# A gMLP and dilated-attention trunk on one core: large-tile subtractions and sums on DVE instead of GpSimd, and the last output weights gated and split ahead

## The chip, the cores and the metric

The kernel runs on one core of a Trainium2 chip. The metric is the device time of one execution, in microseconds, and the time of a kernel is the median of its runs. In the profile the engines are PE (TensorE), DVE (VectorE), ACT (ScalarE), POOL (GpSimd) and SP (SyncE); SP's queue issues all of this kernel's loads and stores.

## What is computed

A residual stream of 2048 tokens by 1024 goes through one gated MLP layer (A) and one layer of dilated attention (B). The reference, cut to the parts that the text speaks of:

```python
def gmlp_layer(x, c, ...):                       # layer A
    h = rms_norm(x, norm_g) * (1 + scale) + shift
    u, v, z = jnp.split(h @ w_in, 3, axis=-1)    # 3 x 2048 columns
    u = jax.nn.gelu(u)
    v = rms_norm(jax.nn.gelu(v), sgu_g)
    mixed = jnp.einsum('gts,bcsge->bctge', w_causal, v) + b_s   # chunks of 128
    y = u * mixed * jax.nn.silu(z)
    return x + gate * (y @ w_out)

def dilated_layer(x, c, kv_groups, ...):         # layer B
    h = rms_norm(x, norm_g) * (1 + scale) + shift
    qz = h @ w_in                                # 24 query heads of 128, and z
    for g, (window, d) in enumerate(((128, 1), (512, 4), (2048, 16))):
        o, lse = dilated_group_attn(q[g], kb[g], vb[g], slopes[g], window, d)
    alpha = jax.nn.softmax(jnp.stack(lses), axis=0)
    y = jnp.sum(alpha * o, axis=0) * jax.nn.silu(z)
    return x + gate * (y @ w_out)
```

Each band of attention sees 256 keys: the 128 of its own block up to the diagonal, and the 128 of the block before from the diagonal on.

## The kernel before

Every large product is made of two fp32r parts of each operand. A weight tile of 128x512 is loaded (256 KB), ACT copies it to the high part (`split`, L255) and DVE or POOL subtracts that from the original to get the low part (L259); high and low lie side by side in one slot of the weight pool, eight slots in all. A product is then three matmuls, high·high, high·low and low·high (`mm3`, L303 to L305; L343 to L345 for the feature-major blocks).

The 2048 tokens run in four quarters of 512, Q = 0 to 3. In each, layer A makes the blocks v (4), u (8) and z (8), the spatial mix, and the output product; then `proj_B` makes the keys and values (kv, blocks 2, 1, 0), the queries (q blocks 2, 1, 0) and z of layer B, with the parts of attention that need later tokens deferred. The q and z blocks, and the output product of Q = 1 to 3, go through `dense_s`, which makes one 2x2 block product from seven smaller ones instead of eight. For that it needs sums and differences of weights and of activations: `combine_weights` (L398) and `combine_out` (L350) make those of the weights once and keep them in DRAM (`wt`, `wq`); `make_ops` (L622) and the class `OutOperands` (L891) make those of the activations in each quarter. In the output product the order of the seven products is 11, s2, 12, s3, s1, 22, s4, and their operands are built shortly ahead of them.

Two of the four combined output weights (`wq`, i = 1 and 2) are kept split for every second row block: in Q = 0's output stage `combine_out` writes the halves into a slot of the weight pool (`wso`, L381 and L382) and stores 512 KB to `wqs`; the later output stages load these with one 512 KB transfer and no split. The other row blocks are loaded raw.

Work that belongs to no block of its own is written as generators, "fillers", which are advanced a step at a time between matmuls (`tick`, at a rate): the sums for the gates, `combine_weights`, the norm of the next quarter, and attention. During layer A of Q = 1 to 3 the filler is `attend_local(Q - 1, wrap=True)`: the 128x256 probabilities of two heads make one chunk (`pr`), with the columns of the block before and of the own block. In a wrapped unit the two halves are folded: POOL multiplies the previous half by the identity (`dg`, L1176), blanks it at and under the diagonal (L1177) and adds it to the own half (L1179); PE transposes the sum (L1196); DVE separates the two halves by a triangular mask out of PSUM (L1200, L1202), and POOL adds the diagonal back (L1203). There are 76 such chunks.

At the end `finish` runs: in the last z block (Q = 3) the fillers are `first()`, which makes the weights of the three groups and prepares the first output tile (`prepare(0)`), and `both()`, which loads layer B's output weights in 16 tiles (`rawo`) and splits them on ACT and POOL (L1293, L1294) into four large tiles `wo`. `prepare` scales and adds the three groups' outputs (DVE and ACT, L1279 to L1347) and multiplies by silu(z) (POOL, L1348). The final loop takes 16 tiles of 128 tokens: transposes (`make_yb`), two products of 24 matmuls (`pf`), then DVE multiplies the result by the gate row `gb` (L1416) and POOL adds the residual (L1417). The attention of Q = 3 is its filler.

A scheduler lists the instructions of each engine; each engine then runs its own list in order, so an instruction that waits holds up all behind it on that engine. All transfers stand on SP's queue, at most eight at a time: each issue also waits for the landing of the one eight before it.

The functions that the change touches, as they were before:

## Time and profile before

| | us |
|---|---|
| median of 3 runs | 3057.24 |
| lowest and highest run | 3051.16, 3058.77 |
| the profiled execution, its own time | 3056.17 |
| its span on the core | 3054.5 |
| PE busy in the span | 2944.3 |
| DVE busy | 2101.4 |
| ACT busy | 1668.5 |
| POOL busy | 1053.1 |

A row of the groups names the line, engine, operation, the tile written and those read, the count, then busy us and mean ns of one, then the idle time of the engine before these instructions and what ended it. In the waits, "PE pp L1196 <- POOL pr L1179: 8.0, 7, 1.5" says that PE's instruction of L1196 waited 8.0 us in all for POOL's of L1179, 7 times, 1.5 us at the longest. The granted clock is TensorE's, as a share of full speed.

### The profile page before, as it was taken

The page shows a single profiled execution, that of the slowest core. Times are in us where ns is not written, and L with a number is a line of the kernel's source. Part 1 is how long each engine was busy: PE and PEld are TensorE (multiplying, and loading weights), DVE is VectorE, ACT ScalarE, POOL GpSimd, SP SyncE. Part 2 cuts the span into 40 slices and gives each one's busy share as a digit, 9 for nine tenths or more (in the row PEclk, how much of TensorE's full clock was granted, in tenths as well). Part 3 has the DMA queues.
Part 4 walks back from the last instruction along what each step waited for, and adds up shares of the span by engine and source line. Part 5 has one row for each costly group of instructions (what it writes and reads, how often), then busy time and mean ns, then how long its engine had stood idle before and what let it go on. Part 6 is the DMA issues. An engine that isn't in the chain of part 4 may idle for free. (4 is left out here: it accounts for less than half of the span.)

```text
span 3054.5 us, 45565 instructions
## 1 busy us (share of the span) xinstructions
PE 2944.3 (96%) x14784; PEld 2465.7 (81%) x14784; DVE 2101.4 (69%) x3596; ACT 1668.5 (55%) x3398; POOL 1053.1 (34%) x1248
## 2 busy tenths in 40 slices
PE   5999989999999999999999999999999999988999
PEld 4788868788888778778888788888888788877887
DVE  6787557673468777765577776856577777767772
ACT  4323336557456555566465565566465568766540
POOL 4147354330025423433144423424145231144322
PEclk8999999999999999999999999999999999999999
DMA  7899677674433577663433676743334666778752
GB/s 235 266 310 343 236 264 258 222 246 125 139 101 116 192 251 237 219 208 104 146 94 121 195 249 206 260 155 117 120 108 135 227 218 218 224 231 290 232 166 92
DMA packets 364227, 601.33 MB, mean 197 GB/s; under 512 B 38378, under 2 KB 137932, under 8 KB 363988
## 3 DMA queue, kind: packets, MB, share of 16 engines
q1 hardware_dynamic: 363988, 598.41, 60.1%
q8 instruction: 117, 1.92, 0.3%
q14 instruction: 122, 1.00, 0.1%
HBM read 478.08 MB, written 120.20 MB: 196 GB/s over the span
## 5 line engine op out<-in xcount | busy, mean ns | idle before, releaser
L305 PE MATMUL pd_v<-w_v,hAh 128*128 128x512 f32 x1024 | 331.5, 405 | 1.2 <-ACT hAh L583 1.2
L305 PE MATMUL pd_kv<-w_kv,hkh 128*128 128x512 f32 x768 | 243.5, 397 | 5.3 <-DVE w_kv L259 4.5
L305 PEld LDWEIGHTS pd_v<-w_v,hAh 128*128 128x128 f32 x1024 | 190.3, 193 | 39.5 <-issue 1.7
L1168 ACT ACTIVATE pr<-pr,stat,rt 128x256 f32<-128x256 f32 (+1 forms) x320 | 177.4, 556 | 64.4 <-DVE stat L1162 36.2
L343 PE MATMUL pd_u<-hAh,w_u 128*128 128x512 f32 x512 | 206.1, 402 | 0.0
L343 PE MATMUL pd_z<-hAh,w_z 128*128 128x512 f32 x512 | 204.3, 399 | 0.0
L305 PE MATMUL pd_v<-w_v,hAl 128*128 128x512 f32 x512 | 203.9, 398 | 0.0
L345 PE MATMUL pd_u<-hAh,w_u 128*128 128x512 f32 x512 | 200.2, 391 | 1.6 <-DVE w_u L259 1.6
L345 PE MATMUL pd_z<-hAh,w_z 128*128 128x512 f32 x512 | 200.0, 391 | 0.0
L344 PE MATMUL pd_u<-hAl,w_u 128*128 128x512 f32 x512 | 199.6, 390 | 0.0
L344 PE MATMUL pd_z<-hAl,w_z 128*128 128x512 f32 x512 | 199.4, 390 | 0.0
L255 ACT ACTIVATE w_u<-raw_u 128x512 fp32r<-128x512 f32 x128 | 79.0, 628 | 184.7 <-PE pd_u L345 100.1
L305 PEld LDWEIGHTS pd_kv<-w_kv,hkh 128*128 128x128 f32 x768 | 145.6, 190 | 38.4 <-DVE w_kv L259 6.6
L1176 POOL TENSOR_TENSOR dg<-pr,ident 128x256 f32<-128x256 f32 x76 | 59.8, 787 | 330.0 <-ACT pr L1168 270.7
L1229 PEld LDWEIGHTS po<-kv,pT 128*128 128x128 f32 x1200 | 147.2, 191 | 8.4 <-ACT pT L1079 2.4
L305 PE MATMUL pd_kv<-w_kv,hkl 128*128 128x512 f32 x384 | 151.8, 396 | 1.0 <-DVE hkl L612 1.0
L1229 PE MATMUL po<-kv,pT 128*128 128x128 f32 x1200 | 149.7, 275 | 1.5 <-ACT pT L1079 1.5
L1014 POOL TENSOR_SCALAR s_q<-s_q 128x4 f32<-128x4 f32 x96 | 24.5, 255 | 362.0 <-DVE s_q L1013 333.4
L259 DVE TENSOR_TENSOR w_u<-raw_u,w_u 128x512 fp32r<-128x512 f32 x128 | 99.4, 787 | 72.0 <-ACT w_u L255 68.5
L1158 DVE SCALAR_TENSOR_TENSOR pr<-dist,rt,ps 128x256 f32<-128x256 f32 (+1 forms) x320 | 122.8, 430 | 34.7 <-PE ps L1155 24.6
L255 ACT ACTIVATE w_z<-raw_z 128x512 fp32r<-128x512 f32 x128 | 77.9, 625 | 123.3 <-PE pd_z L345 49.1
L259 DVE TENSOR_TENSOR w_o<-raw_o,w_o 128x512 fp32r<-128x512 f32 x104 | 92.6, 910 | 53.3 <-ACT w_o L255 53.1
(781 smaller groups left out, 8330.5 us busy)
## 6 DMA issues: line engine op xcount, KB each, us to landing
raw_q<-in_b_w_in_dram SPq DMA_DIRECT2D x144, 256.0 KB, 3.7
raw_v<-in_a_w_in_dram SPq DMA_DIRECT2D x128, 256.0 KB, 3.7
raw_u<-in_a_w_in_dram SPq DMA_DIRECT2D x128, 256.0 KB, 3.9
raw_z<-in_a_w_in_dram SPq DMA_DIRECT2D x128, 256.0 KB, 3.0
raw_o<-in_a_w_out_dram SPq DMA_DIRECT2D x104, 256.0 KB, 3.3
qt<-qd SPq DMA_DIRECT2D x96, 260.0 KB, 3.0
od<-ot SPq DMA_DIRECT2D x96, 256.0 KB, 3.9
raw_kv<-in_w_kv_dram SPq DMA_DIRECT2D x76, 256.0 KB, 3.9
```

What stands on the lines that cost most here:

```text
L255: nc.scalar.activation(hi, src, AF.Copy)
L259: e.tensor_tensor(lo, src, hi.bitcast(F32), ALU.subtract)
L305: last_mm[0] = nc.tensor.matmul(pt, a, u[:, w, :], start=f, stop=e, skip_group_check=more)
L343: nc.tensor.matmul(pts[i], wh, hh[:, k, :], start=k == 0, stop=False)
L344: nc.tensor.matmul(pts[i], wh, hl[:, k, :], start=False, stop=False)
L345: nc.tensor.matmul(pts[i], wl, hh[:, k, :], start=False, stop=k == KT - 1)
L1014: nc.gpsimd.tensor_scalar(s4[:, 4:8], s4[:, 0:4], 1.0 / P, EPS, ALU.mult, ALU.add)
L1158: nc.vector.scalar_tensor_tensor(pr[:, i, :], dist[:, 256 - w:256], u["rt"][:, h:h + 1], psc[:, i, :], ALU.mult, ALU.add)
L1168: nc.scalar.activation(pr[:, i, :], pr[:, i, :], AF.Exp, bias=mneg[:, i:i + 1], scale=u["rt"][:, h:h + 1], accum_out=lsum[:, i:i + 1])
L1176: nc.gpsimd.tensor_tensor(dg, prev, ident.unsqueeze(1).broadcast_to([P, hp, P]), ALU.mult)
L1229: nc.tensor.matmul(po[:, h * P:(h + 1) * P], u["pT"][h // hp][:, h % hp, j, :], u["kv"][:, j, kh, 1, :], start=j == 0, stop=j == nk - 1)
```

## The change

1. Large-tile subtractions, sums and products go from POOL to DVE: those of `combine_out` (32), `combine_weights` (64), `OutOperands` (30 low parts and 48 sums), `make_ops` (28 and 8), 24 of `norm_T`'s low parts, the 18 weight splits that POOL had in the output stages, the scaling of `o1` in attention (32), and the product with silu(z) in `prepare` (16). What POOL keeps are column operations of one to four elements a row, and the large ones of the opening.
2. In the wrapped attention unit the mask is gone: DVE adds the whole previous half to the own half, then makes `dg`; after the transposes DVE subtracts `dg` from the masked half before it takes the difference.
3. The combined output weights are no longer kept split: `wso` and `wqs` are gone, and the later output stages load all of `wq` raw, eight more splits in each.
4. `gate_out`, woven into the attention filler of Q = 2's layer A, loads the 16 tiles of layer B's output weights, multiplies them by the gate row on DVE, splits them (ACT, DVE) into slots of the weight pool and stores them to DRAM (`wob`, 16 transfers of 512 KB). `finish` then only loads them (`load_wo`): the first half ahead of the last q block, the second in a hook behind the fifth product of the last z block. The final loop's gate product is gone, and DVE adds the residual out of PSUM in one operation.
5. In the last z block `first()` is stretched with idle steps, and the first output tile's transposes (`opening`, `make_yb(0)`) are called inside the last product.

The diff, cut to its core:

```diff
-        split(u[:, 0, :], u[:, 1, :], raw, ordered or pool)
+        split(u[:, 0, :], u[:, 1, :], raw, ordered)
...
-        return [split_unit(rows_of(wq2[i], k // 2), f"{nm}{k}") if i in wq2 and k % 2 == 0 else
-                raw_unit(rows_of(wq[i], k), f"{nm}{k}", pool=i not in wq2 and k % 3 == 1)
-                for k in range(KT)]
+        return [raw_unit(rows_of(wq[i], k), f"{nm}{k}") for k in range(KT)]
...
             for i, t in enumerate((t1, t2, t3, t4)):
-                if k % 2 or i not in wq2:
-                    pending.append((rows_of(wq[i], k), t))
-                else:
-                    u = wp.tile([P, 2, 512], F32R, tag="w", name=f"wso{k}{i}")
-                    nc.scalar.activation(u[:, 0, :], t, AF.Copy)
-                    nc.gpsimd.tensor_tensor(u[:, 1, :], t, u[:, 0, :].bitcast(F32), ALU.subtract)
-                    pending.append((rows_of(wq2[i], k // 2), u.bitcast(F32)))
+                pending.append((rows_of(wq[i], k), t))
...
+    def gate_out():
+        items = [(n, k) for n in range(2) for k in range(KT)]
+        gb, raws, us = {}, {}, {}
+        for i in range(len(items) + 2):
...
+                raws[i] = rp.tile([P, 512], F32, tag="raw", name=f"rawo{n}{k}")
+                nc.sync.dma_start(raws[i], b_w_out[k * P:(k + 1) * P, n * 512:(n + 1) * 512])
...
+                    nc.sync.dma_start(wob[n][:, k * P:(k + 1) * P, :].rearrange("e p n -> p e n"),
+                                      us.pop(i - 2).bitcast(F32))
...
+                u = us[i - 1] = wp.tile([P, 2, 512], F32R, tag="w", name=f"w_go{n}{k}")
+                nc.vector.tensor_tensor(raw, raw, gb[n], ALU.mult)
+                nc.scalar.activation(u[:, 0, :], raw, AF.Copy)
+                nc.vector.tensor_tensor(u[:, 1, :], raw, u[:, 0, :].bitcast(F32), ALU.subtract)
...
-                nc.gpsimd.tensor_tensor(r0, r0, h0, ALU.subtract)
+                nc.vector.tensor_tensor(r0, r0, h0, ALU.subtract)
...
-                self.put("12", j, r1, nc.gpsimd if j % 4 else nc.vector)
-                nc.gpsimd.tensor_tensor(r1, r1, self.sums.pop(j), ALU.subtract)
+                self.put("12", j, r1)
+                nc.vector.tensor_tensor(r1, r1, self.sums.pop(j), ALU.subtract)
...
-                nc.gpsimd.tensor_tensor(dg, prev, ident.unsqueeze(1).broadcast_to([P, hp, P]), ALU.mult)
-                nc.gpsimd.affine_select(prev, prev, pattern=[[0, hp], [1, P]], compare_op=ALU.is_gt,
-                                        fill=0.0, base=0, channel_multiplier=-1)
-                nc.gpsimd.tensor_tensor(own, own, prev, ALU.add)
+                nc.vector.tensor_tensor(own, own, prev, ALU.add)
+                nc.vector.tensor_tensor(dg, prev, ident.unsqueeze(1).broadcast_to([P, hp, P]), ALU.mult)
...
+                nc.vector.tensor_tensor(pT[:, :, 1, :], pT[:, :, 1, :], u["dg"][:, c * hp:(c + 1) * hp, :],
+                                        ALU.subtract)
                 nc.vector.tensor_tensor(pT[:, :, 0, :], pc, pT[:, :, 1, :], ALU.subtract)
-                nc.gpsimd.tensor_tensor(pT[:, :, 0, :], pT[:, :, 0, :], u["dg"][:, c * hp:(c + 1) * hp, :], ALU.add)
...
-            scale_heads(nc.gpsimd, u["o1"], u["o1"], e1)
+            scale_heads(nc.vector, u["o1"], u["o1"], e1)
...
-            nc.gpsimd.tensor_tensor(y, y, og["z"], ALU.mult)
+            nc.vector.tensor_tensor(y, y, og["z"], ALU.mult)
...
+        load_wo(0)
+        yield
+        fillers.append(first())
         rate[0] = 4.8
-        yield
+
+        def opening():
+            drain()
+            make_yb(0)
+
+        yield {"hooks": {4: lambda: load_wo(1)}, "mid": opening}
...
-                nc.vector.tensor_tensor(o_, pt, gb[n], ALU.mult)
-                nc.gpsimd.tensor_tensor(o_, o_, xr, ALU.add)
+                nc.vector.tensor_tensor(o_, pt, xr, ALU.add)
```

**How the order moves.** Three places. The first is a wrapped attention unit in Q = 1's layer A. On POOL, before: `dg`, the mask and the sum of two chunks, the scaling of `o1`, then the diagonal.

```order
L1176 TENSOR_TENSOR dg_1_0_7774<-pr_1_00_7760,ident 128x256
L1177 AFFINE_SELECT pr_1_00_7760<-pr_1_00_7760 128x2x128
L1179 TENSOR_TENSOR pr_1_00_7760<-pr_1_00_7760 128x2x128
L1176 TENSOR_TENSOR dg_1_0_7774<-pr_1_01_7779,ident 128x256
L1177 AFFINE_SELECT pr_1_01_7779<-pr_1_01_7779 128x2x128
L1179 TENSOR_TENSOR pr_1_01_7779<-pr_1_01_7779 128x2x128
L1279 TENSOR_TENSOR st_o_0_7906<-st_o_0_7906,stat_185 128x512
L1203 TENSOR_TENSOR pT_1_00_7913<-pT_1_00_7913,dg_1_0_7774 128x2x128
L1203 TENSOR_TENSOR pT_1_01_7917<-pT_1_01_7917,dg_1_0_7774 128x2x128
```

On DVE, before, the masked evacuations stand alone between weight splits (`w_z`):

```order
L259 TENSOR_TENSOR w_z_8187<-raw_z_8188,w_z_8187 128x512
L1200 TENSOR_TENSOR pT_1_00_7913<-pp_1_0_7908,upto 128x2x128
L1202 TENSOR_TENSOR pT_1_00_7913<-pp_1_0_7908,pT_1_00_7913 128x2x128
L1200 TENSOR_TENSOR pT_1_01_7917<-pp_1_0_7908,upto 128x2x128
L1202 TENSOR_TENSOR pT_1_01_7917<-pp_1_0_7908,pT_1_01_7917 128x2x128
L259 TENSOR_TENSOR w_z_8219<-raw_z_8220,w_z_8219 128x512
```

On DVE, after, the sums and `dg` stand between the spatial mix's evacuations (`mt`):

```order
L259 TENSOR_TENSOR w_z_8059<-raw_z_8060,w_z_8059 128x512
L827 SCALAR_TENSOR_TENSOR mt_1_6991<-pm_12_7787,colsb,b_s 128x512
L1209 TENSOR_TENSOR pr_1_00_7736<-pr_1_00_7736 128x2x128
L1210 TENSOR_TENSOR dg_1_0_7750<-pr_1_00_7736,ident 128x256
L827 SCALAR_TENSOR_TENSOR mt_1_6991<-pm_13_7796,colsb,b_s 128x512
L1209 TENSOR_TENSOR pr_1_01_7754<-pr_1_01_7754 128x2x128
L1210 TENSOR_TENSOR dg_1_0_7750<-pr_1_01_7754,ident 128x256
```

and the evacuation, some rows on, has three steps a chunk:

```order
L259 TENSOR_TENSOR w_z_8157<-raw_z_8158,w_z_8157 128x512
L1231 TENSOR_TENSOR pT_1_00_7887<-pp_1_0_7882,upto 128x2x128
L1233 TENSOR_TENSOR pT_1_00_7887<-pT_1_00_7887,dg_1_0_7750 128x2x128
L1235 TENSOR_TENSOR pT_1_00_7887<-pp_1_0_7882,pT_1_00_7887 128x2x128
L1231 TENSOR_TENSOR pT_1_01_7891<-pp_1_0_7882,upto 128x2x128
L1233 TENSOR_TENSOR pT_1_01_7891<-pT_1_01_7891,dg_1_0_7750 128x2x128
L259 TENSOR_TENSOR w_z_8189<-raw_z_8190,w_z_8189 128x512
L1235 TENSOR_TENSOR pT_1_01_7891<-pp_1_0_7882,pT_1_01_7891 128x2x128
```

What was a POOL list of its own now stands in DVE's list; the mask and the last addition are gone, and a subtraction stands in the middle of the evacuation.

The second place is the end of the last z block (`z3b`). On SP, before, the loads of the output weights (`rawo`) alternate with the block's last weights:

```order
L264 DMA raw_z3bt_2_26195<-wt_3_118 128x512
L264 DMA raw_z3bt_3_26200<-wt_3_118 128x512
L1291 DMA rawo_26220<-in_b_w_out_dram 128x512
L1291 DMA rawo_26230<-in_b_w_out_dram 128x512
L264 DMA raw_z3b_0_26247<-in_b_w_in_dram 128x512
L264 DMA raw_z3b_1_26252<-in_b_w_in_dram 128x512
L264 DMA raw_z3b_2_26257<-in_b_w_in_dram 128x512
L264 DMA raw_z3b_3_26262<-in_b_w_in_dram 128x512
L1291 DMA rawo_26274<-in_b_w_out_dram 128x512
L251 DMA zd<-zb_2_26178 128x512
L251 DMA zd<-zb_3_26180 128x512
L1291 DMA rawo_26284<-in_b_w_out_dram 128x512
```

On SP, after, behind the weights of the sixth product (`raw_z3bt`), the second half of the ready output weights (`wo`, 512 KB each) and the z stores stand ahead of the last product's raw weights (`raw_z3b`):

```order
L1323 DMA wo_26228<-wob_124 128x2x512
L251 DMA zd<-zb_0_26113 128x512
L251 DMA zd<-zb_1_26115 128x512
L1323 DMA wo_26228<-wob_124 128x2x512 x2
L1323 DMA wo_26229<-wob_124 128x2x512 x3
L1323 DMA wo_26228<-wob_124 128x2x512
L1323 DMA wo_26229<-wob_124 128x2x512
L251 DMA zd<-zb_2_26240 128x512
L251 DMA zd<-zb_3_26242 128x512
L264 DMA raw_z3b_0_26299<-in_b_w_in_dram 128x512
L264 DMA raw_z3b_1_26304<-in_b_w_in_dram 128x512
L264 DMA raw_z3b_2_26309<-in_b_w_in_dram 128x512
```

On PE, after, the transposes of the first output tile (`pyb`), an attention unit's (`pk`, `pq`) and matmuls of the first output (`pf`) follow the sixth product and stand ahead of the last (`pd_z3ba`):

```order
L303 MATMUL pd_z3bb_25959<-w_z3bt_3_26261,hob_21898 128x512 x3
L1400 MATMUL pyb_0_26345<-ident,og_0_26044 128x128 x4
L1400 MATMUL pyb_1_26352<-ident,og_0_26044 128x128 x4
L1140 MATMUL pk_12_26412<-ident,kv_12_26405 128x128 x2
L1441 MATMUL pf_0_26398<-wo_25193,yb_26344 128x512
L1442 MATMUL pf_0_26398<-wo_25194,yb_26344 128x512
L1140 MATMUL pk_12_26412<-ident,kv_12_26405 128x128 x2
L1150 MATMUL pq_12_0_26420<-ident,qt_12_0_26408 128x128
L1443 MATMUL pf_0_26398<-wo_25193,yb_26344 128x512
L1441 MATMUL pf_0_26398<-wo_25193,yb_26344 128x512
L1442 MATMUL pf_0_26398<-wo_25194,yb_26344 128x512
L1443 MATMUL pf_0_26398<-wo_25193,yb_26344 128x512
```

Before, they stood behind it.

The third place is Q = 0's output stage. On ACT, before, between the copies of the weights (`w_o`) and the residual's squares (`xo`):

```order
L255 ACTIVATE w_o_1_7_3132<-raw_o_1_7_3133 128x512
L381 ACTIVATE wso_3149<-co0pT_3001 128x512
L856 ACTIVATE xo_0_0_3207,sq_0_2928<-xr_0_2920 128x512
L856 ACTIVATE xo_0_1_3213,sq_1_2929<-xr_1_2922 128x512
L381 ACTIVATE wso_3152<-co0pr_2999 128x512
L255 ACTIVATE w_o_0_0_3281<-raw_o_0_0_3282 128x512
```

On ACT, after:

```order
L255 ACTIVATE w_o_1_7_3132<-raw_o_1_7_3133 128x512
L255 ACTIVATE w_o_0_0_3275<-raw_o_0_0_3276 128x512
L884 ACTIVATE xo_0_0_3201,sq_0_2928<-xr_0_2920 128x512
L884 ACTIVATE xo_0_1_3207,sq_1_2929<-xr_1_2922 128x512
L255 ACTIVATE w_o_0_1_3280<-raw_o_0_1_3281 128x512
```

The copies into `wso` are gone from the list, with the slots that they took.

More of the change, by code (lines that the diff above doesn't have):

```diff
@@ L68, in trunk @@
     wq = [dp.tile([D, 512], F32, name=f"wq{i}") for i in range(4)]
-    wq2 = {i: dp.tile([512, 2, 512], F32, name=f"wqs{i}") for i in (1, 2)}
+    wob = [dp.tile([2, D, 512], F32, name=f"wob{n}") for n in range(2)]
     wk2 = {n: dp.tile([512, 2, 512], F32, name=f"wk{n}") for n in (1, 2)}
@@ L927, in build @@
                 r0, r1, h0, h1 = self.quads(j)
[L928 to L929 removed]
+                self.put("s3", j, r0)
+                nc.vector.tensor_tensor(h0, h0, h1, ALU.add)
                 yield
@@ L1051, in proj_B @@
         q_block(1)
+        if Q == NQ - 1:
+            fin = ahead()
+            next(fin)
         q_block(0)
         if Q == NQ - 1:
-            ahead()
-        z_block(0)
+            drain()
+            z_block(**next(fin))
+        else:
+            z_block()
     stat = [cp.tile([P, 16, 16], F32, name=f"stat{g}") for g in range(3)]
@@ L1353, in first @@
         def first():
+            yield from idle(3)
             yield from weights(0, NT - TPQ)
-            ogs[0] = load(0)
-            yield
-            yield
-            yield
+            yield from idle(2)
             ys[0] = prepare(0, ogs[0])
```

113 lines of the change are left out of this document (62 added, 51 removed).

## Prediction

> **What bounds the kernel now.** First the page: the span and the busy times.
>
> ```profile
> span 3054.5 us, 45565 instructions
> PE 2944.3 (96%) x14784; PEld 2465.7 (81%) x14784; DVE 2101.4 (69%) x3596; ACT 1668.5 (55%) x3398; POOL 1053.1 (34%) x1248
> ```
>
> PE is the bound, and the change removes none of its matmuls. Only PE's idle time, 3054.5 − 2944.3 = 110.2 us, and the time it runs at a lowered clock can be won. The waits of PE say what ended the idle stretches:
>
> ```profile
> PE pp L1196 <- POOL pr L1179: 8.0, 7, 1.5
> PE pt_b L605 <- DVE xr L863: 6.7, 8, 3.0
> ...
> PE pd_kv L305 <- DVE w_kv L259: 4.5, 3, 2.0
> ...
> PE pd_o L305 <- ACT w_o L255: 4.3, 1, 4.3
> ...
> PE pd_o2a L305 <- DMA w_o2t<-wqs: 2.7, 2, 1.4
> PE pd_o1b L305 <- DMA w_o1t<-wqs: 2.6, 4, 1.1
> ...
> PE pd_o3b L305 <- DMA w_o3t<-wqs: 2.0, 3, 0.7
> ```
>
> The same view between 2690 and 2790 us, the last z block and the start of the final loop:
>
> ```profile
> PE pd_z3bb L305 <- DVE st_z3bu L500: 4.7, 1, 4.7
> PE pf L1411 <- ACT yb L1372: 4.1, 1, 4.1
> PE pd_z3bb L305 <- ACT w_z3bt L255: 2.5, 1, 2.5
> PE pd_z3bb L305 <- DVE st_q30u L500: 1.7, 1, 1.7
> PE pd_z3ba L305 <- ACT st_z3bu L509: 1.4, 1, 1.4
> ```
>
> Then busy time by stretch (columns: length; busy us and count of PE, weight load, DVE, ACT, POOL; granted clock; DMA share and rate). The rows are the opening; a q stage of quarter 0; the first and second half of quarter 1's output stage; a stretch in quarter 0's output stage; two wrapped attention units; and the two stalls at the end of the last z block.
>
> ```profile
> 0.00:76.40 76.40, 45.53 (x180) 37.66 (x181) 46.42 (x65) 34.62 (x72) 31.48 (x59) 0.89 0.72 235
> 551.60:589.70 38.10, 38.10 (x169) 31.53 (x169) 25.41 (x41) 25.09 (x52) 10.99 (x23) 1.00 0.64 203
> 1007.40:1049.00 41.60, 39.15 (x169) 31.11 (x167) 39.40 (x38) 25.42 (x50) 27.70 (x17) 1.00 0.61 202
> 1049.00:1090.00 41.00, 40.22 (x182) 32.66 (x183) 27.39 (x45) 18.61 (x36) 9.54 (x11) 1.00 0.71 231
> 411.00:440.00 29.00, 25.23 (x100) 20.27 (x101) 16.56 (x24) 10.97 (x22) 17.44 (x16) 0.83 0.78 270
> 1345.00:1360.00 15.00, 12.86 (x61) 10.35 (x60) 7.58 (x17) 9.73 (x21) 5.16 (x9) 0.89 0.17 51
> 2005.00:2020.00 15.00, 12.81 (x60) 10.18 (x59) 8.47 (x21) 10.10 (x21) 5.57 (x8) 0.89 0.17 52
> 2735.00:2742.20 7.20, 4.81 (x12) 3.83 (x13) 7.20 (x7) 3.35 (x7) 6.03 (x3) 0.53 0.73 215
> 2769.00:2776.20 7.20, 5.72 (x15) 4.22 (x16) 4.45 (x6) 5.49 (x15) 0.67 (x1) 0.53 0.93 361
> ```
>
> The opening holds 76.4 − 45.5 = 30.9 us of the idle time, waits for the column sums that the change leaves alone; 79.3 us remain. After a stall of some us the clock is granted at about half for the next 7 us: 7.2 × (1 − 0.53) = 3.4 us lost at each of the last two rows, 29 × 0.17 = 4.9 us at 411, 15 × 0.11 = 1.65 us in each of the two units. So a stall costs more than the wait's row says.
>
> **What moving work from POOL to DVE costs.** The spread of DVE's two-input subtractions, and of the pair L1347/L1348 (min/median/max in ns), then groups of the wrapped attention units (busy us, mean ns):
>
> ```profile
> L259 DVE TENSOR_TENSOR w_o1t<-raw_o1t,w_o1t x18: 680/694/1789, 1014.5 to 1065.1; 128x512 fp32r<-128x512 f32 x18
> ...
> L259 DVE TENSOR_TENSOR w_q01t<-raw_q01t,w_q01t x16: 679/693/695, 548.5 to 575.9; 128x512 fp32r<-128x512 f32 x16
> ```
> ```profile
> L1347 DVE TENSOR_TENSOR og<-og,og x16: 1209/1218/2885, 2734.5 to 2975.2; 128x1024 f32<-128x1024 f32 x16
> ```
> ```profile
> L1348 POOL TENSOR_TENSOR og<-og,zt x16: 2355/2396/3162, 2736.2 to 2979.0; 128x1024 f32<-128x1024 f32 x16
> ```
> ```profile
> L1203 POOL TENSOR_TENSOR pT<-pT,dg 128x256 f32<-128x256 f32 x76 | 63.3, 836 | 114.1 <-DVE pT L1202 101.6 <-DVE sqv L787 4.9 <-PE ps L1155 3.1
> L1179 POOL TENSOR_TENSOR pr<-pr 128x256 f32<-128x256 f32 x76 | 63.2, 831 | 6.3
> L1176 POOL TENSOR_TENSOR dg<-pr,ident 128x256 f32<-128x256 f32 x76 | 59.8, 787 | 330.0 <-ACT pr L1168 270.7 <-DVE stat L1188 50.7 <-DVE stat L1165 6.6
> ...
> L1177 POOL TENSOR_SCALAR_AFFINE_SELECT pr<-pr 128x256 f32<-128x256 f32 x76 | 34.1, 448 | 5.6
> ```
> ```profile
> L1200 DVE TENSOR_TENSOR pT<-pp,upto 128x256 f32<-128x256 f32 x76 | 31.5, 415 | 25.6 <-PE pp L1196 25.5
> ```
>
> The same subtraction takes 0.69 us in the q stage, never over 0.695, and up to 1.79 in the output stage. ACT is as busy in both stretches (25.09, 25.42) and the DMA share alike (0.64, 0.61); what differs is POOL, 10.99 us of small column work against 27.70 us in 17 large tensor operations, 1.6 us each. I take it that these large POOL operations stretch DVE's. The Trainium skill, "SBUF — State Buffer", section "SBUF: two separate sides", says that DVE and GpSimd share one port pair as an exclusive lock, held for a whole instruction, against a DVE operation with two SBUF inputs; the 1.79 us agree. By that rule the small POOL operations that stay would hold DVE too: up to 10.99 us more in the q stage (25.41 + 10.99 = 36.4 of 38.1), so that a stage with added DVE work would pass its length and the sum would be some us smaller, an estimate from this page. The row of 695 ns, with 23 POOL operations beside it, shows no such hold, and my sum has none.
>
> The order of the changed program gives DVE 584 more instructions: 228 of 128x256, 340 of 128x512 and 16 of 128x1024. At 0.42 (L1200), 0.69 and 1.22 us (L1347) that is 96 + 235 + 20 = 351 us. Without any relief DVE would stand at 2101 + 351 = 2452 us, 80% of the span: over the whole it doesn't become the bound. It can in a stage, so stages decide.
>
> **The last z block and the join.** PE's five waits between 2690 and 2790 us are 4.7 + 4.1 + 2.5 + 1.7 + 1.4 = 14.4 us, with two clock losses of 3.4: 21.2 us. What DVE did there:
>
> ```profile
> 2734.52 1.52 DVE L1347 TENSOR_TENSOR og<-og,og 128x1024 f32<-128x1024 f32 x1 [5.92 <-ACT og L1345]
> 2735.96 0.68 DVE L259 TENSOR_TENSOR w_z3bt<-raw_z3bt,w_z3bt 128x512 fp32r<-128x512 f32 x1
> 2736.56 1.27 DVE L500 TENSOR_TENSOR st_z3bu<-pd_z3bb,st_z3bu 128x512 f32<-128x512 f32 x2
> 2737.76 3.34 DVE L259 TENSOR_TENSOR w_z3bt<-raw_z3bt,w_z3bt 128x512 fp32r<-128x512 f32 x2
> ```
>
> DVE stood 5.92 us before an operation of the first output tile, with the evacuation and the splits that PE wanted behind it, and then the splits were stretched by POOL. The change spreads that tile's steps over the whole block, takes the 16 splits of the output weights away from ACT and POOL, and puts the first tile's transposes and seven of its matmuls ahead of the last product. What is late next: the second half of the ready weights, eight loads of 512 KB, stands on SP's queue ahead of the last product's four raw loads. At the 361 GB/s of the row 2769 that is 4.2 MB, 11.6 us, about one of the block's seven products; the pulled work covers only a part. I leave 5 us of loss: **−16** (between −21 and 0).
>
> **The wrapped units.** In each of 76 chunks POOL did L1176, L1177, L1179 in a row, 0.79 + 0.45 + 0.83 = 2.07 us, before PE could transpose; DVE now does the sum first, 0.42 us. Later POOL's 0.84 (L1203) becomes 0.42 on DVE. PE's waits for L1179 are 8.0 us and two units lose 1.65 us of clock each: 11.3 us. The new sum waits for ACT's exponentials in DVE's queue, with weight splits and the spatial mix's evacuation behind it, and PE wants those. I keep 2 us of loss: **−9** (−11 to +10, the upper end being 0.3 us per chunk).
>
> **Quarter 0's output stage.** ACT waited for this:
>
> ```profile
> 411.08 1.67 ACT L255 ACTIVATE w_o<-raw_o 128x512 fp32r<-128x512 f32 x3 [8.99 <-DMA wqs<-wso]
> ```
>
> A weight slot was held by the store of a split combined weight; those stores go. The 4.3 us wait for w_o goes, and half of the 4.9 us of clock: **−7** (−9 to −4).
>
> **The later output stages.** The 7.3 us of waits for wqs (2.7 + 2.6 + 2.0) go with the 512 KB loads; eight raw loads per stage come, each with a copy on ACT and a subtraction on DVE. DVE in the first half is the question:
>
> ```profile
> 1039.70 1.28 DVE L907 TENSOR_TENSOR yos<-mt,yos 128x512 fp32r<-128x512 f32 x2
> ```
>
> Two undisturbed operations take 1.28, 0.64 each in a run. Before: 38 operations, 39.40 us of 41.60. After: 38, the 17 of POOL and 8 splits, 63 × 0.64 = 40.3 us. So DVE gains nothing here; it does POOL's work in the same time. It is 97% full, yet the second half has 41 − 27.4 = 13.6 us free for the operands that are due later. **−3** in all three (−7 to +12).
>
> **The rest.** Waits of kv and pt_b (4.5 + 6.7 us, with the rest of the clock at 411) follow DVE work in stages where POOL's large operations go: **−3** (−8 to 0). In the final loop the end of the chain loses POOL's addition:
>
> ```profile
> 3044.78 1.28 POOL L1417 TENSOR_TENSOR of<-of,xr 128x512 f32<-128x512 f32 x1 [4.16 <-DVE of L1416]
> ```
>
> That is −1.3; **−1** with the rest of the loop, where DVE gains y·z (16 × 1.22 us) and loses its stretching. The gated weights in quarter 2's layer A add 16 × 2 × 0.69 = 22 us on DVE, 16 copies on ACT and 16 stores of 512 KB out of the weight slots, which is just what held quarter 0: **+3** (0 to +20, the upper end three stalls of 4.3 us and their clock).
>
> The sum is −16 − 9 − 7 − 3 − 3 − 1 + 3 = −36. The profiled execution took 3056.17 us, 1.67 around its span, and the median 3057.24 is 1.07 away: 3056.2 − 36 gives **3020 us**.
>
> **Rivals.** *DVE becomes the bound of the output stages, slower.* If DVE's operations stay long without POOL, or come in an order with waits, 39.40 + 17 × 0.69 + 8 × 1.1 (the mean of a lengthened split, between 0.69 and 1.79) = 59.9 us stand in 41.6: +18 in each of three stages. With 20 us won elsewhere: 3056 + 55 − 20 = 3091. It decides from a mean of 41.6/63 = 0.66 us per operation, and outweighs the gains from 0.87. The q stage's 695 ns speak against it, the 97% for it. 8%.
>
> *No change.* POOL's work had its own queue; on DVE each moved step waits in line. If each of the 76 chunks costs PE 0.47 us, the 36 us are gone: 3056. The 5.92 us of L1347 show what such a wait does; for the chunks only the 8 us to be won count against. The Trainium skill, "Perfetto Trace Analysis", section "Optimizing Scalar/DVE Operations", says that moving operations between GpSimd and DVE might not help, since they share a read port; by it the time stays at 3056. The halved durations (2.40 on POOL against 1.22 on DVE) do not bear that out. 10%.
>
> *More.* If the stretching also lies behind stalls that the waits put down to others, three quarters of the 79.3 us and of the 15 us of clock losses counted above (6.8 + 4.9 + 3.3) go: 3056 − 71 = 2985. 10%.
>
> **Numbers.** The forecast has 72%, between 2995 and 3045. A measurement of this kernel can tell about 0.3%, 9 us, from no change: faster 0.72 + 0.10 = 0.82, same 0.10, slower 0.08. The range 2990 to 3054 leaves out half of the third rival, the first, and half of the second: 18%.
>
> **What would show it.** Right: no L259 over 0.8 us outside the opening; no PE wait for L1209's sum over 1 us; no stall at 411; the last z block under 50 us with less than 6 us of PE idle; DVE between 69% and 80% of the span. Wrong: DVE over 95% in an output stage with PE waiting for operands; waits for weights behind stores of the gated tiles in quarter 2; the last product waiting for its raw loads.

## The result and the profile after

The changed kernel takes 3012.52 us, median of 4 runs (3005.81 to 3017.57), against 3057.77 (4 runs) before: a ratio of 0.9855, 95% interval 0.9829 to 0.9882. That is 45 us, 1.5%. The forecast was 36. The profiled execution took 3017.57 us, the slowest of the four; its span and busy times from the page:

```profile
span 3015.4 us, 44951 instructions
...
PE 2933.6 (97%) x14784; PEld 2465.6 (82%) x14784; DVE 2177.0 (72%) x4180; ACT 1682.0 (56%) x3416; POOL 305.5 (10%) x588
```

POOL lost 748 us of busy time and DVE gained 76, with 584 instructions more: what DVE took over costs 351 us by the forecast's durations, so by that count some 275 us of stretching went. The spread of DVE's subtractions (min/median/max in ns) says the same; 1789 has become 695:

```profile
L259 DVE TENSOR_TENSOR w_q<-raw_q,w_q x144: 678/686/695, 465.0 to 2683.6; 128x512 fp32r<-128x512 f32 x144
...
L259 DVE TENSOR_TENSOR w_o1t<-raw_o1t,w_o1t x32: 685/692/695, 1004.2 to 1054.4; 128x512 fp32r<-128x512 f32 x32
```

PE's waits after, the longest:

```profile
PE pc_a L779 <- DVE acc_a L775: 23.4, 4, 17.5
...
PE pp L1242 <- ACT pr L1201: 4.7, 3, 3.1
PE pd_z3ba L303 <- ACT w_z3b L255: 4.3, 1, 4.3
PE pp L1242 <- DVE b_s L1191: 4.2, 2, 2.4
PE pd_z1bb L303 <- DVE st_z1bu L532: 3.8, 1, 3.8
PE pd_z2ba L303 <- DVE w_z2bt L259: 3.6, 1, 3.6
PE pq L1150 <- DMA qt<-qd: 2.8, 1, 2.8
PE pt_b L637 <- DVE xr L891: 2.8, 6, 0.8
```

The opening's wait stands as it was. The waits for POOL's sum, for `wqs`, and the 4.3 us in quarter 0's output stage are gone. New in the list are waits in z blocks (`z1b`, `z2b`) that had almost none.

Where the time went is best seen in the lengths of the blocks, each from the start of its first matmul to that of the next block's, in us, read off the two traces:

| blocks | before | after | difference |
|---|---|---|---|
| output stage, Q0 | 100.8 | 88.9 | −11.9 |
| output stages, Q1, Q2, Q3 | 83.2, 82.5, 82.3 | 79.2, 79.0, 78.4 | −11.4 |
| first two kv blocks, Q0 to Q3 | 50.2, 57.3, 46.7, 47.0 | 46.4, 50.2, 46.3, 46.1 | −12.2 |
| v and u of Q1 to Q3 (wrapped attention) | 712.8 | 697.6 | −15.2 |
| last z block and all behind it | 342.0 | 325.2 | −16.8 |
| z block, Q0, Q1, Q2 | 42.3, 41.6, 40.7 | 51.3, 46.9, 47.2 | **+20.8** |
| Q3, last kv block and q block behind it | 131.7 | 140.8 | +9.1 |
| everything else | | | −1.5 |

The rows add up to the spans' difference, 3054.5 − 3015.4 = 39.1 us. So the gains were 67 us and more, and 30 were given back at places that the forecast did not name. Each column is one execution, and the traces of the experiments below, read the same way, show how far a block that an edit leaves alone still varies: v and u of Q1 to Q3 take 696.6 to 702.6 us with the changed units, and the three z blocks 138.5 to 145.4 together with the changed order, so their loss is 14 to 21 us.

### The profile page after: what moved, and what is told of

The parts are those of the page before. It is cut to its first block, busy times and chain, and to the rows that moved or that the text cites. A ratio compares the mean times of both kernels' runs of the same rounds, so it can differ in the third digit from the quotient of the medians.

```text
span 3015.4 us, 44951 instructions
## 1 busy us (share of the span) xinstructions
PE 2933.6 (97%) x14784; PEld 2465.6 (82%) x14784; DVE 2177.0 (72%) x4180; ACT 1682.0 (56%) x3416; POOL 305.5 (10%) x588
## 5 line engine op out<-in xcount | busy, mean ns | idle before, releaser
L1191 DVE SCALAR_TENSOR_TENSOR pr<-dist,rt,ps 128x256 f32<-128x256 f32 (+1 forms) x320 | 124.6, 432 | 23.9 <-PE ps L1182 11.9
L259 DVE TENSOR_TENSOR w_u<-raw_u,w_u 128x512 fp32r<-128x512 f32 x128 | 87.1, 687 | 61.6 <-ACT w_u L255 61.4
L255 ACT ACTIVATE w_q<-raw_q 128x512 fp32r<-128x512 f32 x144 | 88.6, 627 | 75.4 <-DMA raw_q<-in_b_w_in_dram 46.8
L237 POOL TENSOR_SCALAR r_b<-sq 128x1 f32<-128x1 f32 x16 | 6.1, 383 | 1196.0 <-DVE sq L889 1195.9
L259 DVE TENSOR_TENSOR w_q<-raw_q,w_q 128x512 fp32r<-128x512 f32 x144 | 95.7, 687 | 41.4 <-ACT w_q L255 40.6
```

Source lines behind the costliest of these rows:

```text
L255: nc.scalar.activation(hi, src, AF.Copy)
L259: e.tensor_tensor(lo, src, hi.bitcast(F32), ALU.subtract)
L1191: nc.vector.scalar_tensor_tensor(pr[:, i, :], dist[:, 256 - w:256], u["rt"][:, h:h + 1], psc[:, i, :], ALU.mult, ALU.add)
```

## The experiments

Twelve kernels, each compared with the kernel before on its chip. Times are medians of 4 to 6 runs, but for the probe's one.

**The z blocks (norm_pool, q_late).** First the same stretch of quarter 2 on SP's queue, before (start, duration, tile, count): the stores of the last normalised queries (`qd`) between the loads of the z block's weights (`raw_z2b`, `raw_z2bt`).

```profile
1947.36 2.25 SPq L251 DMA_DIRECT2D qd<-st_q20v  x2
1949.71 1.34 SPq L264 DMA_DIRECT2D raw_z2bt<-wt  x3
1951.45 0.33 SPq L264 DMA_DIRECT2D raw_z2b<-in_b_w_in_dram  x1
1954.13 2.25 SPq L251 DMA_DIRECT2D qd<-st_q20w  x2
1956.48 1.34 SPq L264 DMA_DIRECT2D raw_z2b<-in_b_w_in_dram  x3
1957.91 0.38 SPq L264 DMA_DIRECT2D raw_z2bt<-wt  x1
1960.58 2.25 SPq L251 DMA_DIRECT2D qd<-st_q20u  x2
```

After:

```profile
1921.75 2.25 SPq L251 DMA_DIRECT2D qd<-st_q20v  x2
1924.10 1.34 SPq L264 DMA_DIRECT2D raw_z2bt<-wt  x3
1927.55 2.24 SPq L251 DMA_DIRECT2D qd<-st_q20w  x2
1929.89 0.37 SPq L264 DMA_DIRECT2D raw_z2bt<-wt  x1
1930.37 0.87 SPq L264 DMA_DIRECT2D raw_z2b<-in_b_w_in_dram  x2
1932.75 5.08 SPq L251 DMA_DIRECT2D qd<-st_q20u  x2
```

Before, four loads stand between the first and the second pair of stores and four between the second and the third. After there are three and three: the fourth `raw_z2bt` stands behind the second pair and is issued at 1929.89. A q store waits for POOL's column work on its queries, and all loads behind it wait too. SP's own waits in this block, after (us in all, times, longest):

```profile
SPq L251 <- POOL s_q L1042: 6.9, 2, 4.7
SPq L251 <- POOL st_q20u L1045: 5.8, 2, 4.3
```

On ACT and PE after, the load that came late:

```profile
1932.92 0.63 ACT L255 ACTIVATE w_z2bt<-raw_z2bt 128x512 fp32r<-128x512 f32 x1 [2.92 <-DMA raw_z2bt<-wt]
1933.45 0.61 ACT L1039 ACTIVATE hs_q<-st_q20u 128x512 f32<-128x512 f32 x1
```
```profile
1935.51 6.97 PE L303 MATMUL pd_z2ba<-w_z2bt,hob 128*128 128x512 f32 x17 [3.62 <-DVE w_z2bt L259]
```

ACT waits 2.92 us for that load, with the square of the last queries (`hs_q`) behind it, and those queries' store again holds the next loads: the third pair of stores takes 5.08 us with its waits, against 2.25 before. The move that alters this list is that of the next quarter's norm (`norm_T`), which runs as a filler in just these blocks:

```diff
-                e = nc.gpsimd if act else nc.vector
+                e = nc.gpsimd
```

> The changed kernel with the 24 low parts of the norm's filler (norm_T) back on POOL. In the changed kernel's profile the last z blocks of quarters 0 to 2 take 51.3, 46.9 and 47.2 us against 42.3, 41.6 and 40.7 before, and SP waits for POOL's query norms with weight loads queued behind. Theory: the list of SP, which stood otherwise after the move, reads as before again (one weight load more ahead of each pair of q stores); the three blocks go back to 41 to 43 us and the time falls by 15 to 20 us, to about 2994. Rival: the blocks are longer because DVE has more to do in them, or some other moved operation shifted them; then they stay over 45 us or the time moves by less than 5 us.

Measured: 3001.61 us, ratio 0.9818 (0.9796 to 0.9839); the z blocks take 42.2, 41.0 and 41.7 us. The blocks went where the theory put them, and SP's list again has four loads between the pairs of stores. SP waits for POOL there too, 14.5 us in all in quarter 2's block against 17.3 in the changed kernel; what differs is which loads stand behind. The time fell by 11 us between the medians, less than the 15 to 20 expected, and by 24 between the profiled executions; the intervals overlap, so the total is less sure than the blocks. DVE is stretched again there, which costs nothing:

```profile
L259 DVE TENSOR_TENSOR w_z1bt<-raw_z1bt,w_z1bt x16: 673/684/1669, 1259.6 to 1287.7; 128x512 fp32r<-128x512 f32 x16
```

This put both the list and DVE's load back. To tell them apart, the next kernel leaves the norm on DVE and moves the stores alone:

```diff
+        held = []
...
-                pending.append((qd[g][rows(t), n, :], src))
+                (held if g == 0 and Q < NQ - 1 else pending).append((qd[g][rows(t), n, :], src))
...
-            z_block()
+            z_block(hooks={1: lambda: pending.extend(held)})
```

> The changed kernel, norm's low parts on DVE as in the change, but the eight q stores of the first q block of quarters 0 to 2 issued on SP behind the weight loads of the next z block's third product, so that 12 weight loads of that block stand ahead of the last of them (13 before, 10 in the changed kernel). Theory: the place on SP's list makes the z blocks long, not the work on DVE: they go from 51.3, 46.9 and 47.2 us to 41 to 44, as with the norm on POOL (42.2, 41.0, 41.7); the time falls by 10 to 20 us against the changed kernel, to 2993 to 3002. Rival: DVE's added work in the block holds PE; then they stay over 45 us with the loads early.

Measured: 2993.99 us, ratio 0.9796 (0.9779 to 0.9813); z blocks of 41.0, 41.0 and 40.5 us. It was the place on SP's list. SP's wait for POOL's `s_q` is down from 6.9 us to this:

```profile
SPq L251 <- POOL s_q L1046: 0.6, 1, 0.6
```

The same block of quarter 2 by windows, after and in q_late (length; busy us of PE, weight load, DVE, ACT, POOL; granted clock; DMA):

```profile
1925.60:1972.80 47.20, 43.58 (x189) 35.46 (x188) 37.71 (x65) 27.38 (x47) 7.26 (x15) 0.93 0.82 277
```
```profile
1911.40:1951.90 40.50, 40.50 (x190) 33.46 (x189) 33.34 (x57) 24.66 (x43) 7.05 (x11) 1.00 0.86 282
```

With all of the norm on DVE, DVE is busy 33.3 of 40.5 us and PE never stops.

**The output stages (oo_pool).** The operands' low parts and sums back on POOL; the combined weights still all split:

```diff
-                self.put("12", j, r1)
-                nc.vector.tensor_tensor(r1, r1, self.sums.pop(j), ALU.subtract)
+                self.put("12", j, r1, nc.gpsimd if j % 4 else nc.vector)
+                nc.gpsimd.tensor_tensor(r1, r1, self.sums.pop(j), ALU.subtract)
...
```

> The changed kernel with the output operands' low parts and sums on POOL again (30 and 48), all combined weights still split on ACT and DVE. By my sum DVE is as busy with POOL's share as without it, but here eight splits come on top and POOL lengthens them: 39.4 + 8 x 0.69 to 1.1 = 45 to 48 us of work in a first half of 41.6. Theory: the output stages of quarters 1 to 3 go from 79.2, 79.0 and 78.4 us to 82 to 86 each, the time up by 9 to 20 us, to 3022 to 3032. Rival: the second halves have room and the operands are due late enough: under 1.5 us each, under 5 us in all.

Measured: 3024.05 us, ratio 0.9897 (0.988 to 0.9914), 11.5 us over the changed kernel's median; the stages take 82.6, 82.4 and 82.8 us. In the ten other kernels that keep these operations on DVE they take 78.3 to 80.1. The theory's low end. The first half of quarter 1's output stage, in the changed kernel:

```profile
996.00:1037.60 41.60, 41.60 (x185) 34.46 (x184) 39.59 (x65) 31.62 (x60) 0.00 (x0) 1.00 0.58 178
```

and with POOL's share back:

```profile
996.00:1037.60 41.60, 39.44 (x170) 31.06 (x169) 40.99 (x41) 27.18 (x51) 26.41 (x16) 1.00 0.48 141
```

DVE alone does 65 operations in 39.59 us, 0.61 each, and PE doesn't wait. With POOL's 16 beside it, DVE gets 41 done in 40.99. PE waits for splits again:

```profile
PE pd_o1b L303 <- DVE w_o1t L259: 2.1, 2, 1.7
PE pd_o3b L303 <- DVE w_o3t L259: 2.1, 2, 1.7
PE pd_o2a L303 <- DVE w_o2t L259: 2.1, 2, 1.7
```

**Who stretches DVE (probe).** POOL operations on raw tiles after their use are added to the changed kernel, one kind per quarter:

```diff
         split(u[:, 0, :], u[:, 1, :], raw, ordered)
+        if nm[:4] == "q01t":
+            nc.gpsimd.tensor_tensor(raw, raw, raw, ALU.add)
+        elif nm[:4] == "q11t":
+            nc.gpsimd.tensor_scalar(raw, raw, 2.0, None, ALU.mult)
+        elif nm[:4] == "q21t":
+            nc.gpsimd.memset(raw, 0.0)
```

> The changed kernel with added POOL operations on raw weight tiles that have been used: behind each of 16 splits of the second q stage an addition of two inputs in quarter 0, a product with a constant in quarter 1, a fill without an input in quarter 2, nothing in quarter 3, all 128x512. Only the durations of DVE's subtractions in those stages count. Theory: POOL's large operations lengthen DVE's two-input operations: in quarter 0 the splits of that stage go from 0.69 us at most to means over 1 us with maxima of 1.5 to 1.8, in quarter 3 they stay under 0.7; evacuations out of PSUM in the same stage stay at 0.7. Whether the product with one input and the fill do so the theory leaves open; if only reading counts the fill leaves DVE at 0.69. Rival: the lengthening came from something else in the output stages: all stay under 0.75.

Measured (3023.27 us): the splits of that stage, quarters 0, 1 and 2:

```profile
L259 DVE TENSOR_TENSOR w_q01t<-raw_q01t,w_q01t x16: 677/693/1526, 531.8 to 559.9; 128x512 fp32r<-128x512 f32 x16
...
L259 DVE TENSOR_TENSOR w_q11t<-raw_q11t,w_q11t x16: 678/691/1093, 1186.7 to 1214.2; 128x512 fp32r<-128x512 f32 x16
...
L259 DVE TENSOR_TENSOR w_q21t<-raw_q21t,w_q21t x16: 680/692/694, 1852.8 to 1880.2; 128x512 fp32r<-128x512 f32 x16
```

The maximum of quarter 0 is as the theory had it, the mean not (0.93 us): nine of the 16 splits aren't held up by one of POOL's additions, which start when a split ends. The first two that are, on DVE and on POOL:

```profile
533.17 0.99 DVE L259 TENSOR_TENSOR w_q01t<-raw_q01t,w_q01t 128x512 fp32r<-128x512 f32 x1 [0.67 <-ACT w_q01t L255]
534.52 1.30 DVE L259 TENSOR_TENSOR w_q01t<-raw_q01t,w_q01t 128x512 fp32r<-128x512 f32 x1 [0.36 <-ACT w_q01t L255]
```
```profile
532.58 1.04 POOL L269 TENSOR_TENSOR raw_q01t<-raw_q01t 128x512 f32<-128x512 f32 x1 [4.79 <-DVE w_q01t L259]
534.24 1.04 POOL L269 TENSOR_TENSOR raw_q01t<-raw_q01t 128x512 f32<-128x512 f32 x1 [0.63 <-DMA raw_q<-in_b_w_in_dram]
```

POOL's first addition ends at 532.58 + 1.04 = 533.62, DVE's split at 534.16; the second at 535.28, the split at 535.82. Both times DVE ends 0.54 us after POOL, whenever it started: it stands until POOL has about finished. The seven that are lengthened among these splits, and two others beside them, all end 0.54 to 0.55 us after an addition. The kernel before shows the same without a probe: of its 1058 splits on L259, 143 took longer than 0.72 us, and 141 of these began inside an operation of POOL and ended 0.54 to 0.55 us after it. In the changed kernel three such splits are left. A fill without an input doesn't do this (694 ns at most), and a product with one input mostly not:

```profile
1188.02 0.69 DVE L259 TENSOR_TENSOR w_q11t<-raw_q11t,w_q11t 128x512 fp32r<-128x512 f32 x1 [0.67 <-ACT w_q11t L255]
```
```profile
1187.44 2.96 POOL L271 TENSOR_SCALAR raw_q11t<-raw_q11t 128x512 f32<-128x512 f32 x2 [4.80 <-DVE w_q11t L259]
```

This split took 0.69 us beside POOL's two products, whose entry covers both. Four splits in quarter 1's stretch took 1.07 to 1.10 us. They began 1.41 to 1.45 us before the end of a product and ended 0.34 us before it; those that weren't lengthened began 1.02 us or less before a product's end. So the product too held DVE up, but only in its early part.

**Quarter 0's output stage (wso_back).** The split copies of the combined weights back, their subtraction on DVE:

```diff
+                if k % 2 or i not in wq2:
+                    pending.append((rows_of(wq[i], k), t))
+                else:
+                    u = wp.tile([P, 2, 512], F32R, tag="w", name=f"wso{k}{i}")
+                    nc.scalar.activation(u[:, 0, :], t, AF.Copy)
+                    nc.vector.tensor_tensor(u[:, 1, :], t, u[:, 0, :].bitcast(F32), ALU.subtract)
+                    pending.append((rows_of(wq2[i], k // 2), u.bitcast(F32)))
...
```

> The changed kernel with the split combined output weights back in DRAM, the subtraction of the split on DVE. Theory: the store out of the weight slot holds ACT in quarter 0's output stage, whoever subtracts: that stage, 88.9 us in the changed kernel and 100.8 before, goes to 95 to 101, and the later output stages change by less than 1.5 us each (weight waits against eight splits less): 3018 to 3026 in all. Rival: the stage was held by POOL's queue, where the subtraction stood: the stage stays under 92 us and the time within 4 us of the changed kernel's 3012.5.

Measured: 3008.8 us, ratio 0.9842 (0.9823 to 0.9862); the stage stays at 88.9 us. The theory falls, the rival stands: the store out of the slot held ACT only because it came late, and it came late because of POOL's queue. POOL before:

```profile
405.50 1.29 POOL L369 TENSOR_TENSOR co<-co,co 128x512 f32<-128x512 f32 x1 [12.56 <-DMA co<-in_a_w_out_dram]
406.74 1.31 POOL L382 TENSOR_TENSOR wso<-co2pT,wso 128x512 fp32r<-128x512 f32 x1
```

The subtraction into `wso`, whose copy ACT had made at 395.4, stood in POOL's list behind a combination (L369) that waited 12.56 us for its loads. In wso_back ACT's copy began at 393.0 and DVE followed at once:

```profile
393.64 0.69 DVE L383 TENSOR_TENSOR wso<-co2pT,wso 128x512 fp32r<-128x512 f32 x1 [6.85 <-ACT wso L382]
```

The later output stages took 79.1, 78.4 and 78.5 us, as in the changed kernel, and PE has no wait for `wqs`, with the 512 KB loads back. So the 7.3 us of waits for `wqs` before were not the price of these loads either.

**The wrapped units (wrap_pool).** The folding of `att_2` and the diagonal of `att_3` as before, on POOL:

```diff
-                nc.vector.tensor_tensor(own, own, prev, ALU.add)
-                nc.vector.tensor_tensor(dg, prev, ident.unsqueeze(1).broadcast_to([P, hp, P]), ALU.mult)
+                nc.gpsimd.tensor_tensor(dg, prev, ident.unsqueeze(1).broadcast_to([P, hp, P]), ALU.mult)
+                nc.gpsimd.affine_select(prev, prev, pattern=[[0, hp], [1, P]], compare_op=ALU.is_gt,
+                                        fill=0.0, base=0, channel_multiplier=-1)
+                nc.gpsimd.tensor_tensor(own, own, prev, ALU.add)
...
-                nc.vector.tensor_tensor(pT[:, :, 1, :], pT[:, :, 1, :], u["dg"][:, c * hp:(c + 1) * hp, :],
-                                        ALU.subtract)
                 nc.vector.tensor_tensor(pT[:, :, 0, :], pc, pT[:, :, 1, :], ALU.subtract)
+                nc.gpsimd.tensor_tensor(pT[:, :, 0, :], pT[:, :, 0, :], u["dg"][:, c * hp:(c + 1) * hp, :], ALU.add)
```

> The changed kernel with the wrapped attention unit as before (identity product, mask, sum and diagonal on POOL). Theory: POOL's three operations in a row are late for PE: v and u of quarters 1 to 3, 697.6 us together in the changed kernel and 712.8 before, go back by 9 to 15 us, with PE waiting for POOL's sum again for 6 to 9 us, and the time rises as much, to 3021 to 3028. Rival: PE waited there since DVE's operations were lengthened by other POOL work: under 4 us.

Measured: 3020.27 us, ratio 0.9883 (0.9866 to 0.99), 8 us over the changed kernel; v and u of quarters 1 to 3 take 706.2 us, 8.6 more. PE waits for POOL's sum again, for half of what it was before:

```profile
PE pp L1229 <- POOL pr L1212: 3.9, 4, 1.5
```

The size is unsure: the changed unit has 696.6 to 702.6 us in these blocks in the other kernels, which makes the unit worth 4 to 10 us, and the intervals of the two times overlap. Theory and rival both hold in part. With POOL's other large work gone, the fold on POOL still makes PE wait, but only half as long, which points to that other work for the other half of the 8.0 us. The rest of the 15.2 us in these blocks came with the rest of the change.

**The end (join_old, wo0_late, wo1_late).** First the old end: raw output weights split in the last z block, `finish` as before, no `gate_out`.

```diff
-            fillers.append(weave(main, gate_out()) if Q == 2 else main)
+            fillers.append(main)
...
-        load_wo(0)
-        yield
-        fillers.append(first())
+        fs = first()
+        def both():
+            yield from w_out(0)
+            yield from w_out(1)
+        fillers.extend([fs, both()])
...
```

> The changed kernel with the end as before: raw output weights split in the last z block on ACT and POOL, the product with silu(z) and the residual's addition on POOL, the gate in the final loop, no gated weights in quarter 2. Theory: the stretch from the last z block to the end, 325 us in the changed kernel and 342 before, goes back to 338 to 342, less up to 3 us for the gated weights that quarter 2 no longer makes: the time rises by 11 to 17 us, to 3024 to 3030. Rival: the gain at the end came from POOL's large operations elsewhere being gone, and the new loads do little: a rise of 5 us or less.

Measured: 3027.47 us, ratio 0.99 (0.9883 to 0.9917), 15 us over the changed kernel. The end took 338.3 us against 325.2 (from the z block's first matmul at 2683.1 to the span's 3021.4). v and u of quarter 2 took 237.8 us without the gated weights, 238.8 with them in the changed kernel, and 237.8 to 242.2 in the other kernels that have both them and the changed units: `gate_out` costs between nothing and 4 us. Then the place of the first half's loads:

```diff
         q_block(1)
-        if Q == NQ - 1:
-            fin = ahead()
-            next(fin)
         q_block(0)
         if Q == NQ - 1:
+            fin = ahead()
+            next(fin)
```

> The changed kernel with the first half of the ready output weights (8 loads of 512 KB) loaded at the start of the last z block, not beside the q blocks before it. In the changed kernel the last kv block and the q block behind it take 41.6 + 99.2 = 140.8 us against 131.7 before, with 4.2 MB more to load there. Theory: those loads delay attention's loads of q; without them the two take 132 to 135 us, and the last z block and what follows to the end (321.4 us) get longer by 0 to 12, since DMA is busy there: the time between 3003 and 3020. Rival: the two blocks are longer for another reason, and stay over 138 us.

Measured: 3008.24 us, ratio 0.9852 (0.9828 to 0.9875). The two blocks took 135.9 us. But they took 133.8 to 138.9 in the other variants of the changed kernel (135.6 in join_old, which does not load there), so 140.8 was a high draw and these loads aren't the cause. What makes the two blocks longer than the 131.7 of before stays open. And the second half's loads, on top of q_late:

```diff
-        yield {"hooks": {4: lambda: load_wo(1)}, "mid": opening}
+        yield {"hooks": {6: lambda: load_wo(1)}, "mid": opening}
```

> The kernel q_late with the second half of the ready output weights (8 loads of 512 KB) called behind the last z block's last product instead of two products earlier, so that they stand behind its four raw loads on SP. Theory: in the changed kernel PE waits 4.3 us for ACT's copy of the last product's weights, since those loads stood behind 4.2 MB; the wait and the lowered clock behind it go, and the stretch from the last z block to the end (321.4 us in q_late) falls to 313 to 318: the time against q_late by 3 to 8 us, to 2986 to 2991. Rival: the second half then comes too late for the first tile's second product, whose matmuls PE needs as filling, and PE waits for it as long: 319 to 324 us, within 3 us of q_late.

Measured: 2989.79 us, ratio 0.9782 (0.9764 to 0.98), 4 us under q_late with intervals that overlap. The stretch, taken to the last matmul as that expectation has it, is 318.5 us against 321.4, but norm_pool, without this edit, has 318.8: no gain is shown. The wait for the last weights is gone, another for the first tile's transposed operand has come:

```profile
PE pf L1443 <- ACT yb L1404: 2.5, 1, 2.5
PE pd_z3bb L303 <- DVE st_z3bu L532: 1.2, 1, 1.2
```

**All late stores (q_late_all, both_late, before_late).** The q blocks run in the order 2, 1, 0; q_late holds the stores of block 0, which its expectation calls the first. Now those of block 1, the second, are held as well, and both in quarter 3 too:

```diff
-                pending.append((qd[g][rows(t), n, :], src))
+                (held[g] if g < 2 else pending).append((qd[g][rows(t), n, :], src))
...
+            dense_s(hb, in_blocks(g), f"q{Q}{g}", ev, hooks=release(1) if g == 0 else {})
```

> The kernel q_late with the same for the q stores of the second q block, held until the third product's loads of the first q block are issued, and in quarter 3 too. Theory: what is left of lost time in the first q blocks (42.4 and 41.7 us in quarters 0 and 1, 38.1 to 39.5 in quarter 2) has the same cause, weight loads queued behind q stores that wait for POOL; these two fall to 38 to 40 and the time by 4 to 8 us against q_late, to 2986 to 2990. Rival: those blocks wait for their operands or for the norm of the next quarter, not for loads: within 3 us of q_late, or slower by up to 6 us in quarter 3, where attention reads the stored q.

Measured: 2979.88 us, ratio 0.9752 (0.9734 to 0.9771): 14 us under q_late, more than the theory. The q blocks 0 of quarters 0 and 1 went from 42.4 and 41.7 to 40.2 and 41.1 us only; the last z block and what follows from 325.2 to 320.3, where the held stores of quarter 3 can count. These make 7.7 us; where the rest of the 14 comes from is not shown.

both_late is q_late_all with wo1_late's edit:

```diff
-        yield {"hooks": {4: lambda: load_wo(1)}, "mid": opening}
+        yield {"hooks": {6: lambda: load_wo(1)}, "mid": opening}
```

> The kernel q_late_all with the second half of the ready output weights behind the last product, as in wo1_late. In wo1_late the wait for ACT's copy of the last weights went (4.2 to 0), and the stretch to the end took 318.5 us against 321.4, while a wait for the first tile came (2.5 us). Theory: the two edits touch different waits; against q_late_all (2979.9, with 2.5 us of that wait left) 1 to 4 us less, 2976 to 2979. Rival: with q_late_all the loads at the end already come early enough and the later half costs: 0 to 4 us more.

Measured: 2979.84 us, ratio 0.975 (0.9735 to 0.9764): no difference. before_late is the kernel before the change with the stores held:

```diff
-                pending.append((qd[g][rows(t), n, :], src))
+                (held[g] if g < 2 else pending).append((qd[g][rows(t), n, :], src))
...
-            dense_s(hb, in_blocks(3), f"z{Q}b", ev)
+            dense_s(hb, in_blocks(3), f"z{Q}b", ev, hooks=release(0))
```

> The kernel before the change with the q stores of the first two q blocks held as in q_late_all, nothing else. Theory: it was the change that put weight loads behind these stores; before it the z blocks took 42.3, 41.6 and 40.7 us, so there is little to win: the z blocks at 40.5 to 41.5, the first q blocks 2 us less, and 3 to 8 us in all, 3048 to 3054. Rival: the held stores are a gain of their own, as large as on the changed kernel (33 us from 3012.5 to 2979.9), whatever the engine of the subtractions: under 3040.

Measured: 3041.44 us, ratio 0.9942 (0.9928 to 0.9957), 15 us under the kernel before: between theory and rival. The z blocks of quarters 0 to 2 took 41.0, 41.0 and 40.7; 11 us came in the last z block and behind it, which the theory had left out; PE's wait of 4.7 us for `st_z3bu` is not there any more. Of the 33 us that the held stores save on the changed kernel, some 15 were there to be had before it. In the three z blocks they save 22.9 us on the changed kernel and 1.9 on the kernel before, so most of the rest is what the change's own order had cost.

## Why the prediction was right, point by point

**The number** was near (3020 against 3012.5, inside 2990 to 3054), in part by luck, since two errors met: the gains were larger than forecast and a loss wasn't forecast.

**POOL's large operations stretch DVE's, and DVE doesn't become the bound:** right, and shown by the probe and by oo_pool. DVE stands at 72%, within the 69% to 80%. No split takes over 0.8 us outside the opening.

**The last z block and the join, −16 with the loop's −1:** the stretch fell by 16.8 us; join_old gives 15 back in time. The residue was the one named: the last product waited 4.3 us for weights behind the eight loads of 512 KB. The block's own matmuls span 50.5 us, where under 50 was named as a sign of being right; in the window of them PE is idle for 5.2 us:

```profile
2690.20:2742.00 51.80, 46.59 (x207) 37.56 (x206) 32.41 (x53) 27.13 (x53) 8.00 (x16) 0.93 0.96 338
```

Two terms of the sum were sized badly. The 11.6 us of loads are about one and a half of this block's seven products, not one. And the 3.4 us of lost clock at each of the two stalls count PE's idle part of the 7.2 us a second time; of its 4.81 and 5.72 us at work, 0.47 make 2.3 and 2.7.

**The wrapped units, −9:** the unit alone is worth 4 to 10 (wrap_pool), and the blocks gave 15.2. No wait for L1209's sum appears; the "no change" rival's price per chunk did not come.

**Quarter 0's output stage, −7:** the wait went, 11.9 us in all. The reason was wrong at its root. The forecast had a weight slot held by a store; wso_back keeps slot and store and loses nothing. The store came late since its subtraction had stood behind a waiting combination in POOL's list.

**The later output stages, −3:** mis-sized; they gave 11.4, and oo_pool takes 11.5 back. The step that failed is "DVE gains nothing here": the count was good (40.3 us forecast, 39.59 measured), but the forecast valued a stage only by PE's waits for `wqs`, which go even where the 512 KB loads stay (wso_back). Before, DVE was as busy with fewer operations done, and PE's window had 41.60 − 39.15 = 2.45 us idle, of which the change's stage has none.

**The rest, −3:** the first two kv blocks of the quarters gave 12.2, more than the two waits' 11.2 of which I took a part. No run puts these blocks' operations back alone, so their cause is argued and not shown.

**Gated weights, +3:** between nothing and 4 us (join_old). The reason given for it, stores out of weight slots, was the one that failed for quarter 0.

**What was missing:** a term for the next quarter's norm. Its 24 low parts were in the 351 us of DVE work, and no step asked where SP's list would stand after them. That is the +20.8, or 14 to 21 with the other kernels, shown by norm_pool and q_late. The forecast did read the list of SP at the join, and nowhere else.

**The rivals:** DVE as the bound of the output stages didn't come; at 0.61 us per operation the stage was under the 0.66 from which it would decide. *More* (2985) didn't come in time, though the five places above gained 67 us of its 71; the losses kept it away. The Trainium skill, "Perfetto Trace Analysis", section "Optimizing Scalar/DVE Operations", says that moving operations between GpSimd and DVE might not help. Here such a move alone did: with the output operands back on POOL (oo_pool) the three output stages take 11.2 us more.

## What to carry to other kernels

When two engines hold each other up, moving the slower one's work costs less than its durations say: read what the other's operations take where the first is idle, and put that in the sum. After a change that moves filler work, compare the order of every queue, the DMA queue first: a store that waits for a slow producer holds each load behind it, and here that gave back a fifth to a third of the gain. A wait's row names what came last, not what it would be worth; a stage's length against one without stalls says that better.
